# A macaron encoder layer on one core: the start of the program laid out anew, and a gate's result kept in the tile of its first product

## The chip, the cores and the metric

The kernel runs on one core of one Trainium2 chip. The metric is device microseconds of one execution, from the first to the last instruction plus what lies around them. The engines are named as the profile names them: PE is TensorE's matmul, PEld its weight load, DVE is VectorE, ACT is ScalarE, POOL is GpSimd and SP is SyncE. SP, ACT and POOL also issue the DMA transfers.

## What is computed

```python
def rmsnorm(x, g):
    y = x * lax.rsqrt(jnp.mean(x * x, axis=-1, keepdims=True) + NORM_EPS)
    return y * g

def swiglu(x, w_gate, w_up, w_down):
    return (jax.nn.silu(x @ w_gate) * (x @ w_up)) @ w_down

# one layer, x is 1024 tokens by 1024, float32
h = swiglu(rmsnorm(x, ffn1_pre_g), ffn1_w_gate, ffn1_w_up, ffn1_w_down)   # 2816 wide
x = x + 0.5 * rmsnorm(h, ffn1_post_g)
h = rmsnorm(x, mix_pre_g)
q, k, v = heads(h @ w_qkv)
o = concat(rmsnorm(neighbourhood_attention(...)), rmsnorm(dilated_attention(...)))
x = x + rmsnorm(o @ w_out, mix_post_g)
h = swiglu(rmsnorm(x, ffn2_pre_g), ffn2_w_gate, ffn2_w_up, ffn2_w_down)
x = x + 0.5 * rmsnorm(h, ffn2_post_g)
```

## The kernel before, in words

**Products.** Every float32 product is done as three fp32r products: each operand is split into a rounded part "hi" (a cast on ACT, L355 for weights, L171 for activations) and the rest "lo" (a subtraction on DVE, L356 and L172), and PE adds hi by hi, hi by lo and lo by hi (mm3, L262 to L264). On top of that the big products use a scheme with seven block products in the place of eight. The activations are cut into token halves and model halves (A11 and so on), and sums and differences of the blocks (S1 to S4 on the activations, T1 to T4 on the weights) are formed on DVE. A block product of one chunk is 12 matmuls: four slices of 128 by three products, 512 tokens wide.

**The first feed-forward net.** PairGemm walks over 22 pairs, each 128 columns of the gate matrix and 128 of the up matrix. The first `early` of them (9 in FFN1, 10 in FFN3, which is the second feed-forward net) have their two left products, A11 and A12, done ahead (`ahead`), while the second token half is still being normalised; the partial results go to DRAM through POOL's queue (s1d L428, sgd L543) and come back later. Then `run` takes one pair, b, per turn.

**A plain turn of `run`**, that is one with b at or over `early`, goes like this on PE, whose order is the written one: A11 of b (12 matmuls into bank a); then the last product of b-1, A22 (`last`, L518); then S2 of b, added into the same bank a, from which ACT must first have copied the A11 result (`keep`, L374, tile "s1" of pool sp); then A12 of b, whose result goes to `GatePairs.first`; then S1, S3 and S4. Pool sp has two buffers for the tag "s1". `first` (L533) takes a fresh tile "sg" from pool cp (tag "g1", three buffers, L549), adds A12 and s1 into it on DVE (L537) and applies SiLU on ACT (L539). `second` multiplies (L553) and writes the tile to DRAM (L560). `last` does the same for the other token half (SiLU L565, product L566) and, for odd b, forms four sums out of the tiles of b-1 and b (L574 to L577), of which L576 overwrites the sg tile of b-1 and L577 that of b; five POOL DMAs (L572, L579) then write the blocks to DRAM, in the order A22, S1, S3, S2, S4. S2 lies in the tile of b-1, S4 in that of b.

**Other traffic in a plain turn.** SP loads the weights of the pair after next (L349, L350) and a tile for sums of the down matrix (L318, L319); those sums are formed on DVE (L327 to L329) and written through POOL (L330), one step a turn in the turns 8 to 18.

**The start.** Token tiles 0 to 3 are loaded (L1374), the norm weights are spread to 128 partitions by a POOL DMA (L256), ACT squares and sums (L162), DVE forms the inverse root by three Newton steps from an integer guess (L137 to L148), scales whole tiles of 1024 (L211), PE transposes (L170), and the first product A11 is done for two pairs, in halves of 256 tokens. In this stretch PE, ACT and DVE go in the written order; afterwards only PE does, and a scheduler orders the others.

Of the kernel before, what the change touches and what calls it, by code (L numbers as in the profile page):

```python
# [10 lines left out]
F32 = mybir.dt.float32  # L11
F32R = mybir.dt.float32r
I32 = mybir.dt.int32
AF = mybir.ActivationFunctionType
# [5 lines left out]
P, T = 128, 512  # L20
# [73 lines left out]
class Weights:  # L94
# [64 lines left out]
def sumsq(c, x, ss, junk=None):  # L159
    if junk is None:  # L160
        junk = c.xp.tile([P, T], mybir.dt.bfloat16, tag="junk", name="junk", bufs=1)
    c.nc.scalar.activation(junk[:, :x.shape[-1]], x, AF.Square, accum_out=ss)  # L162
# [12 lines left out]
class Operand:  # L175
# [158 lines left out]
class PairGemm:  # L334
# [190 lines left out]
class GatePairs:  # L525
# [237 lines left out]
    return onehot, lncount, m.reshape(P, 384)  # L763


def build_bias(c, rel, t5, onehot, lncount):

    nc = c.nc
    stk = c.dr.tile([8, 8, 15, 24], F32, name="stk")
    tab = c.dr.tile([2, 8, T], F32, name="tab")  # L770
    t5t = c.bp.tile([32, 8], F32, tag="b0", name="t5t")
    nc.gpsimd.dma_start(t5t, t5.rearrange("h b -> b h"))
    for i in range(2):
        oh = c.bp.tile([P, T], F32, tag="oh", name="oh")
        cols = slice(511 * i, 511 * i + 511)
        nc.gpsimd.dma_start(oh[:32, :511], onehot[:, cols])
        lc = c.bp.tile([P, T], F32, tag="lc", name="lc")
        nc.gpsimd.dma_start(lc[:8, :511], lncount[:, cols].broadcast_to([8, 511]))
        ps = c.pst.tile([P, 4, P], F32, tag="tr", name="tabp").rearrange("p a b -> p (a b)")
        nc.tensor.matmul(ps[:8, :511], t5t, oh[:32, :511], start=True, stop=True)  # L780
        nc.vector.tensor_add(lc[:8, :511], ps[:8, :511], lc[:8, :511])
        nc.gpsimd.dma_start(tab[i, :, :511], lc[:8, :511])
        g = c.gab[i]
        dst = bass.AP(tensor=g.tensor, offset=g.offset, ap=[[P * 640, 8], [641, P], [1, 511]])
        nc.gpsimd.dma_start(dst, tab[i, :, :511].unsqueeze(1).broadcast_to([8, P, 511]))
    neg = c.bp.tile([P, T], F32, tag="oh", name="neg")
    nc.gpsimd.memset(neg[:, :384], NEG)
    nc.gpsimd.dma_start(c.nb.rearrange("h p r e -> p h (r e)"), neg[:, :384].unsqueeze(1).broadcast_to([P, 8, 384]))
    for cc in range(8):
        nc.gpsimd.dma_start(stk[cc], rel[:, :, 7 - cc:31 - cc])  # L790
    for r in range(16):
        r0 = min(max(r - 4, 0), 8)
        nc.gpsimd.dma_start(c.nb[:, r * 8:r * 8 + 8, r0:r0 + 8, :].rearrange("h c r e -> c h (r e)"),
                            stk[:, :, r0 - r + 7:r0 - r + 15, :].rearrange("c h r e -> c h (r e)"))
# [76 lines left out]
class Unit:  # L871
# [21 lines left out]
    def copy(self):  # L893
        c = self.c
        self.pt = c.ptp.tile([P, 4, P], F32, tag="pt", name="pt")
        (c.nc.vector.tensor_copy if self.count % 4 == 3 else c.nc.scalar.copy)(self.pt[:, :self.n], self.tps[:, :self.n])
# [232 lines left out]
class GroupNorm:  # L1129
# [48 lines left out]
def layer(tc, a, out):  # L1178
    nc = tc.nc
    c = Ctx(tc)  # L1180
    with ExitStack() as ctx:
# [184 lines left out]
        with ExitStack() as order:  # L1366
# [4 lines left out]
            def load(ts, queues):  # L1371
                for t, q in zip(ts, queues):
                    xs[t] = c.xp.tile([P, D], F32, tag="x", name="x", bufs=4)
                    q.dma_start(xs[t], x0[t])  # L1374
            xs = {}
            load((0, 1), (nc.sync, nc.scalar))
            op0 = Operand(c, load_gain(c, a["ffn1_pre_g"], "pre"), 0)

            def begin(pg):
                load((2, 3), (nc.scalar, nc.sync))  # L1380

                def drain():
                    while c.sums:
                        c.sums.popleft()()

                def norm(*ts):
                    op0.scale(*n[ts])
                    drain()
                def junk():
                    return c.xp.tile([P, D], F32, tag="s", name="junk", bufs=2)  # L1390
                n = {(0, 1): op0.squares([0, 1], [xs[0], xs[1]], junk())}
                norm(0, 1)
                pg.split_left(0)
                n[2, 3] = op0.squares([2, 3], [xs[2], xs[3]], junk())
                op0.one(0)
                op0.one(1)
                pg.split_left(1)
                acc, s1 = [pg.bank() for _ in range(2)], []
                for b in range(2):
                    pg.mm(acc[b], pg.w[b], 0, A11, cols=slice(0, 256))  # L1400
                op0.one(0)
                norm(2, 3)
                op0.one(2)
                op0.one(3)
                for b in range(2):
                    pg.mm(acc[b], pg.w[b], 0, A11, cols=slice(256, 512))
                    s1.append(pg.save(b, acc[b]))
                    if b:
                        op0.one(1)
                load((4, 5), (nc.gpsimd, nc.gpsimd))  # L1410
                op0.one(2)
                op0.one(3)
                order.close()
                order.enter_context(ordered())
                return s1
            F = lambda *ts: lambda: op0.norm(ts, [xs[t] for t in ts])
# [45 lines left out]
            vp.run(2, 3)  # L1462
            pg.fetch(0)
            pg.fetch(1)
            build_bias(c, a["na_rel_bias"], a["t5_rel_bias"], a["onehot"], a["lncount"])
            vp.run(4, 5)
            pg.begin()
            pg.begin_rest()
# [222 lines left out]
```

## Time and profile before

| | |
|---|---|
| median of 3 runs | 1920.19 us (1920.02 to 1921.11) |
| profiled execution | 1922.76 us, of which the span of instructions is 1921.0 us |
| granted TensorE clock, mean | 0.989 |
| PE busy | 1851.7 us, 96% |
| DVE / ACT / POOL busy | 1313.9 / 799.8 / 311.7 us |
| HBM read / written | 274.84 / 129.50 MB |

A row of a timeline gives start, duration, engine, line, operation, tile written and tiles read, shapes, and in brackets how long the engine sat idle before it and what ended that. A row of a stretch ("A:B") gives its length, then the busy time of PE, PEld, DVE, ACT and POOL with the number of instructions, the granted TensorE clock as a share, the busy share of the DMA engines and GB/s. A DMA row gives the tiles, the queue, the count, the size of one and the us from issue to landing.

### The profile page before, as it was taken

How to read it: one execution, taken by the hardware profiler on the slowest of the kernel's cores; microseconds unless marked ns; L12 is line 12 of the kernel's file. 1: busy time of each engine (PE TensorE's matmuls, PEld its weight loads, DVE VectorE, ACT ScalarE, POOL GpSimd, SP SyncE). 2: the span in 40 equal slices, each digit the busy share in tenths (PEclk: the TensorE clock that was granted, in tenths of full speed). 3: DMA queues.
4: the chain of work that ended last, by engine and by line, in shares of the span. 5: the costliest groups of instructions: out<-in, count | busy, mean ns of one | idle time of the engine just before them, and what ended most of it. 6: DMA issues, size and time to landing. Idle time of an engine off the chain costs nothing.

```text
span 1921.0 us, 25047 instructions
## 1 busy us (share of the span) xinstructions
PE 1851.7 (96%) x9044; PEld 1545.2 (80%) x9044; DVE 1313.9 (68%) x2205; ACT 799.8 (42%) x1287; POOL 311.7 (16%) x504
## 2 busy tenths in 40 slices
PE   5999999999999989999999999989999999999997
PEld 4788888888888867778799987777888888888886
DVE  5778777676565866548566775776788777654557
ACT  4522333334444545224477765453222333344332
POOL 2111111111000122342432310121111111110000
PEclk8999999999999999999999999999999999999999
DMA  6645465645986756866974642483456655476563
GB/s 237 223 159 188 170 222 216 222 167 197 327 273 200 273 193 205 292 198 197 313 265 142 212 159 88 155 301 136 159 192 241 215 195 210 159 275 212 198 229 133
DMA packets 162461, 400.96 MB, mean 209 GB/s; under 512 B 18001, under 2 KB 34561, under 8 KB 160289
## 3 DMA queue, kind: packets, MB, share of 16 engines
q1 hardware_dynamic: 112880, 224.62, 35.3%
q0 software_dynamic: 48592, 172.64, 24.8%
q10 hardware_dynamic: 864, 2.10, 0.3%
q8 instruction: 71, 1.16, 0.2%
q14 instruction: 54, 0.43, 0.1%
HBM read 274.84 MB, written 129.50 MB: 210 GB/s over the span
## 4 chain that ended last, share of the span: by engine, by line
PE 82%; DVE 6%; issue 5%; DMA 4%; ACT 2%; POOL 1%; SPq 0%; DVEq 0%; POOLq 0%; ACTq 0%
PE mmp L264 16%; PE mmp L262 16%; PE mmp L263 16%; PE accp L263 8%; PE accp L262 8%; PE accp L264 8%; PE po L992 3%; PE ptp L891 2%; PE sp L980 2%; PE trp L170 1%; PE po L1113 1%; DMA wraw<-in_wqk_dram 1%; PE sp L1100 1%; DMA x<-x 1%; DMA wraw<-in_wu_dram 1%
## 5 line engine op out<-in xcount | busy, mean ns | idle before, releaser
L262 PE MATMUL mmp<-x,whi 128*128 128x512 f32 (+1 forms) x1464 | 579.8, 396 | 7.6 <-ACT whi L355 3.6
L264 PE MATMUL mmp<-x,wlo 128*128 128x512 f32 (+1 forms) x1464 | 575.5, 393 | 1.0 <-DVE wlo L356 1.0
L263 PE MATMUL mmp<-x,whi 128*128 128x512 f32 (+1 forms) x1464 | 574.8, 393 | 0.5 <-DVE x L172 0.2
L262 PEld LDWEIGHTS mmp<-x,whi 128*128 128x128 f32 x1464 | 278.2, 190 | 67.0 <-ACT whi L355 4.2
L264 PEld LDWEIGHTS mmp<-x,wlo 128*128 128x128 f32 x1464 | 277.9, 190 | 62.3 <-DVE wlo L356 1.9
L263 PEld LDWEIGHTS mmp<-x,whi 128*128 128x128 f32 x1464 | 278.4, 190 | 59.9 <-DVE x L172 1.4
L613 DVE TENSOR_TENSOR pw<-praw,pw 128x1024 fp32r<-128x1024 f32 (+1 forms) x182 | 199.2, 1138 | 122.4 <-ACT pw L612 122.1
L612 ACT CAST pw<-praw 128x1024 fp32r<-128x1024 f32 (+1 forms) x182 | 169.2, 983 | 208.6 <-PE accp L264 168.0
L355 ACT CAST whi<-wraw 128x1024 fp32r<-128x1024 f32 x129 | 135.2, 1050 | 251.6 <-PE mmp L263 213.0
L262 PE MATMUL accp<-pw 128*128 128x512 f32 x600 | 234.4, 391 | 0.0
L264 PE MATMUL accp<-pw 128*128 128x512 f32 x600 | 233.5, 389 | 0.0
L263 PE MATMUL accp<-pw 128*128 128x512 f32 x600 | 233.4, 389 | 0.0
L356 DVE TENSOR_TENSOR wlo<-wraw,whi 128x1024 fp32r<-128x1024 f32 x129 | 157.6, 1225 | 23.6 <-ACT whi L355 23.5
L264 PEld LDWEIGHTS accp<-pw 128*128 128x128 f32 x600 | 112.6, 188 | 23.7
L262 PEld LDWEIGHTS accp<-pw 128*128 128x128 f32 x600 | 112.7, 188 | 23.5 <-issue 0.4
L263 PEld LDWEIGHTS accp<-pw 128*128 128x128 f32 x600 | 112.7, 188 | 23.0
L560 POOL DMA_DIRECT2D g<-sg x44 | 23.9, 542 | 475.2 <-DVE sg L553 304.0
L518 DVE TENSOR_TENSOR c<-mmp,u 128x512 f32<-128x512 f32 x52 | 36.0, 691 | 83.9 <-PE mmp L264 82.8
L374 ACT COPY s<-mmp 128x512 f32<-128x512 f32 x52 | 30.5, 587 | 147.3 <-PE mmp L264 145.7
L355 ACT CAST whi<-traw 128x512 fp32r<-128x512 f32 x52 | 32.3, 621 | 118.2 <-DVE traw L444 59.2
L172 DVE TENSOR_TENSOR x<-trp,x 128x512 fp32r<-128x512 f32 x84 | 57.2, 687 | 34.7 <-ACT x L171 34.7
L443 DVE TENSOR_TENSOR wraw<-wraw 128x1024 f32<-128x1024 f32 x52 | 63.6, 1224 | 24.2 <-DMA wraw<-in_wqk_dram 11.9
(230 smaller groups left out, 2699.8 us busy)
## 6 DMA issues: line engine op xcount, KB each, us to landing
praw<-g SPq DMA_DIRECT2D x70, 512.0 KB
wraw<-in_wg_dram SPq DMA_DIRECT2D x44, 512.0 KB
wraw<-in_wu_dram SPq DMA_DIRECT2D x44, 512.0 KB
tr<-in_wd_dram SPq DMA_DIRECT2D x44, 512.0 KB
g<-sg POOLq DMA_DIRECT2D x88, 256.0 KB, 4.1
ts<-tr POOLq DMA_DIRECT2D x22, 1024.0 KB, 4.7
praw<-ts SPq DMA_DIRECT2D x88, 256.0 KB
praw<-in_wd_dram SPq DMA_DIRECT2D x66, 256.0 KB
```

What stands on the lines that cost most here:

```text
L172: nc.vector.tensor_sub(lo, ps, hi.bitcast(F32))
L262: nc.tensor.matmul(out, ahi, bhi, start=start, stop=False, skip_group_check=go_on)
L263: nc.tensor.matmul(out, ahi, blo, start=False, stop=False, skip_group_check=go_on)
L264: nc.tensor.matmul(out, alo, bhi, start=False, stop=stop, skip_group_check=go_on)
L355: nc.scalar.copy(hi, raw)
L356: nc.vector.tensor_sub(lo, raw, hi.bitcast(F32))
L443: nc.vector.tensor_sub(r[:, 0:2], r[:, 1:3], r[:, 0:2])
L612: nc.scalar.copy(w[side][:, 0, :m], raw[:, :m])
L613: nc.vector.tensor_sub(w[side][:, 1, :m], raw[:, :m], w[side][:, 0, :m].bitcast(F32))
L891: c.nc.tensor.transpose(self.tps[:, j, :], self.probs[:, j * P:(j + 1) * P], c.ident)
L980: nc.tensor.matmul(out, lhs, keys[i], start=i == 0, stop=i == 1)
L992: nc.tensor.matmul(po[0][:, un * 2 + j], u.pt[:, 2 * j + t, :], rhs, start=t == 0, stop=t == 1)
```

## The change

Three things are altered.

1. The start is written out anew (`begin`). The norm weights come as one row of 4 KB and PE spreads them over the partitions by a product with a row of ones (L1402); one of the first two tiles is squared and summed on DVE instead of ACT (L1409); the inverse root is ACT's square root, DVE's reciprocal and one Newton step (L1419 to L1424); tiles are scaled by halves of 512; weights of three pairs instead of two come by halves on SP's queue; three pairs instead of two have their A11 product done here; and the order of PE, ACT and DVE is written down. Token tiles 4 and 5 now come on SP's queue, the copies of xn to DRAM are issued at the end, and the loads of the neighbourhood bias (stk) move from build_bias to turn 1.
2. FFN1 does 10 pairs ahead instead of 9, and the steps of the second token half move one turn later with it.
3. `GatePairs.first` uses the tile s1, where it is given one, as the result tile: `sg = s1 or ...`. It is given one for the pairs begun in the start and in every plain turn of FFN1 and FFN3.

```diff
@@ PairGemm.ahead
             if b + 1 not in self.w:
-                self.split_left(b + 1)
+                if b + 1 == len(begun):
+                    c.behind(lambda: self.split_left(b + 1), DVE, ACT)
+                else:
+                    self.split_left(b + 1)
@@ GatePairs.first
     def first(self, b, ps, keep, s1=None):
         c, nc = self.c, self.c.nc
-        sg = c.sp.tile([P, T], F32, tag="s1", name="sg") if keep else self.tile()
+        sg = s1 or (c.sp.tile([P, T], F32, tag="s1", name="sg") if keep else self.tile())
         if s1 is not None:
             nc.vector.tensor_add(sg, ps, s1)
@@ build_bias
-    stk = c.dr.tile([8, 8, 15, 24], F32, name="stk")
+    stk = c.rel
-    for cc in range(8):
-        nc.gpsimd.dma_start(stk[cc], rel[:, :, 7 - cc:31 - cc])
@@ ffn
-                pg.start()
@@ layer, the start
-            load((0, 1), (nc.sync, nc.scalar))
-            op0 = Operand(c, load_gain(c, a["ffn1_pre_g"], "pre"), 0)
+            op0 = Operand(c, None, 0)
             def begin(pg):
...
+                nc.sync.dma_start(row[:1, :D], a["ffn1_pre_g"])
+                load((0, 1), (nc.sync, nc.scalar))
+                fetch(0, 0)
                 load((2, 3), (nc.scalar, nc.sync))
+                for b, i in ((1, 0), (2, 0), (0, 1), (1, 1), (2, 1)):
+                    fetch(b, i)
+                nc.vector.memset(row[:1, D:], 1.0)
+                nc.vector.memset(eps, EPS)
+                nc.scalar.activation(ss[:, 2:3], eps[:, 0:1], AF.Sqrt)
+                for g, copy in enumerate((nc.scalar.copy, nc.vector.tensor_copy)):
+                    ps, sl = pg.bank(), slice(g * T, g * T + T)
+                    nc.tensor.matmul(ps, row[:1, D:], row[:1, sl], start=True, stop=True)
+                    copy(op0.gain[:, sl], ps)
...
+                def square_here(t):
+                    nc.vector.tensor_tensor_reduce(out=xn[t], in0=xs[t], in1=xs[t], scale=1.0, scalar=0.0,
+                                                   op0=ALU.mult, op1=ALU.add, accum_out=ss[:, t:t + 1])
+                def root(t):
+                    x = ss[:, t:t + 2]
...
+                    nc.scalar.activation(q, x, AF.Sqrt, bias=eps[:, 0:1], scale=1.0 / D)
+                    nc.vector.tensor_scalar(h, x, -0.5 / D, -0.5 * EPS, op0=ALU.mult, op1=ALU.add)
+                    nc.vector.reciprocal(y, q)
+                    nc.vector.tensor_mul(e, y, h)
+                    nc.vector.tensor_mul(e, e, y)
+                    nc.vector.scalar_tensor_tensor(y, e, 1.5, y, op0=ALU.add, op1=ALU.mult)
...
+                square(0)
+                square_here(1)
+                root(0)
+                whigh(0, 0)
+                scale(0, 0)
+                scale(1, 0)
+                turn(0, 0)
+                turn(1, 0)
...
+                products(2, (2,), every)
+                low(3, 1)
+                wlow(0, 1)
+                s1.append(pg.save(2, acc[2]))
+                for b in (1, 2):
+                    whigh(b, 1)
+                    wlow(b, 1)
+                save(0, 1, 2, 3)
+                pg.fetch_left(3)
+                pg.fetch_left(4)
...
-            op, fin, hs, prep = ffn(1, op0, prep, gate_pairs(1, op0, a["wg1"], a["wu1"], 9), get1,
-                                    {0: [F(4, 5), L(6, 7)], 2: [U(4)], 3: [F(6, 7), U(5)], 5: [U(6)], 6: [U(7)]},
+            op, fin, hs, prep = ffn(1, op0, prep, gate_pairs(1, op0, a["wg1"], a["wu1"], 10), get1,
+                                    {0: [lambda: c.behind(F(4, 5), ACT), L(6, 7)], 1: [rel], 3: [U(4)], 4: [F(6, 7), U(5)], 6: [U(6)], 7: [U(7)]},
```

How the order moves. On ACT, from turn 11's copy of v to turn 12's, before: s_2308 is the copy of A11 of b = 12, c_2322 the SiLU in `last` of b = 11, u_2355 the copy after S2. "waits" names what an instruction waits for; the DMASW entries are transfers that POOL issued.

```order
L374 COPY v<-mmp 128x512 [waits PE_49]
L355 CAST whi<-traw 128x512 [waits DVE_49,Activation_49]
L355 CAST whi<-wraw 128x1024 [waits DMAHW6_49,PE_49,Activation_49]
L374 COPY s_2308<-mmp 128x512 [waits PE_49]
L355 CAST whi<-wraw 128x1024 [waits DVE_49,PE_49,Activation_49]
L565 ACTIVATE c_2322<-c_2322 128x512 [waits DVE_49]
L374 COPY u_2355<-mmp 128x512 [waits PE_49]
```

The same stretch now, in which s_2340 is the copy of A11 of b = 12 and c_2354 the SiLU in `last` of b = 11:

```order
L374 COPY v<-mmp 128x512 [waits PE_49]
L355 CAST whi<-traw 128x512 [waits DVE_49,Activation_49]
L355 CAST whi<-wraw 128x1024 [waits DMAHW5_49,PE_49,Activation_49]
L355 CAST whi<-wraw 128x1024 [waits DVE_49,PE_49,Activation_49]
L568 ACTIVATE c_2354<-c_2354 128x512 [waits DVE_49]
L374 COPY s_2340<-mmp 128x512 [waits DMASW2_49,DVE_49]
L374 COPY u_2387<-mmp 128x512 [waits PE_49]
```

The copy has moved behind the SiLU of the pair before, and it waits for a DVE instruction and for a POOL transfer. The copies of b = 14, 16, 18 and 20 in FFN1, and of b = 12 to 20 by twos in FFN3, stand the same way; those of odd b stand where they stood.

On POOL, the writes that end the pair of b = 10 and 11, and the first ones after them, before (sg is the tile from pool cp):

```order
L572 DMA g_6_169<-c_2267 128x512 [waits DMASW0_49,DVE_49]
L579 DMA g_2_165<-s_2334 128x512 [waits DMASW1_49,DVE_49]
L579 DMA g_5_168<-c_2133 128x512 [waits DMASW2_49,DVE_49]
L579 DMA g_1_164<-sg 128x512 [waits DMASW3_49,DVE_49]
L579 DMA g_3_166<-sg 128x512 [waits DMASW4_49,DVE_49]
```

and now, where s_2064 and s_2207 are the A11 copies of b = 10 and 11:

```order
L575 DMA g_6_163<-c_2299 128x512 [waits DMASW7_49,DVE_49]
L582 DMA g_2_159<-s_2366 128x512 [waits DMASW0_49,DVE_49]
L582 DMA g_5_162<-c_2166 128x512 [waits DMASW1_49,DVE_49]
L582 DMA g_1_158<-s_2064 128x512 [waits DMASW2_49,DVE_49]
L582 DMA g_3_160<-s_2207 128x512 [waits DMASW3_49,DVE_49]
```

The writes stand in the same order; the fourth and fifth now read the tiles of tag "s1". A POOL transfer takes the numbered slot whose last use it waits for, so DMASW2, for which s_2340 waits, is the write of s_2064.

More of the change, by code (lines that the diff above doesn't have):

```diff
@@ L1375, in layer @@
             xs = {}
-            load((0, 1), (nc.sync, nc.scalar))
-            op0 = Operand(c, load_gain(c, a["ffn1_pre_g"], "pre"), 0)
+            op0 = Operand(c, None, 0)
             def begin(pg):
-                load((2, 3), (nc.scalar, nc.sync))
[L1382 to L1412, printed above, removed]
@@ new lines, in begin, with fetch @@
+                row, eps, ss = c.xp.tile([P, D + P], F32, tag="s", name="row", bufs=2), *[
+                    c.small.tile([P, 4], F32, tag=t, name=t) for t in ("eps", "ss")]
+                raw, xn, got, acc, s1 = [None] * 3, [None] * 4, {}, [], []
+                def fetch(b, i):
+                    if raw[b] is None:
+                        where = dict(tag="x1", bufs=c.deep) if b == 2 else dict(tag="g")
+                        raw[b] = (c.xp if b == 2 else c.wg).tile([P, 2, T], F32, name="graw", **where)
+                        pg.w[b] = [c.wr.tile([P, 2, T], F32R, tag="g" + p, name="w" + p) for p in ("hi", "lo")]
+                    nc.sync.dma_start(raw[b][:, i], pg.srcs[b][0][:, i * T:(i + 1) * T])
@@ new lines, in begin @@
+                nc.sync.dma_start(row[:1, :D], a["ffn1_pre_g"])
+                load((0, 1), (nc.sync, nc.scalar))
+                fetch(0, 0)
+                load((2, 3), (nc.scalar, nc.sync))
+                for b, i in ((1, 0), (2, 0), (0, 1), (1, 1), (2, 1)):
[3 more added lines that the diff above has]
+                nc.scalar.activation(ss[:, 2:3], eps[:, 0:1], AF.Sqrt)
+                op0.gain = c.xp.tile([P, D], F32, tag="pre", name="gain", bufs=1)
@@ new lines, in place @@
+                def place(t):
+                    where = dict(tag="x1", bufs=c.deep) if t == 3 else dict(tag="xn", bufs=c.xn)
+                    xn[t] = c.xp.tile([P, D], F32, name="xn", **where)
+                def root(t):
+                    x = ss[:, t:t + 2]
+                    q, h, y, e = [c.small.tile([P, 4], F32, tag=n, name=n)[:, :2] for n in ("q0", "v", "y", "e")]
+                    nc.scalar.activation(q, x, AF.Sqrt, bias=eps[:, 0:1], scale=1.0 / D)
[4 more added lines that the diff above has]
+                    nc.vector.scalar_tensor_tensor(y, e, 1.5, y, op0=ALU.add, op1=ALU.mult)
+                    r.update({t + i: y[:, i:i + 1] for i in range(2)})
@@ new lines, in begin, with scale, save, turn @@
+                r = {}
+                def scale(t, g):
+                    sl = slice(g * T, g * T + T)
+                    nc.vector.scalar_tensor_tensor(xn[t][:, sl], xs[t][:, sl], r[t], op0.gain[:, sl],
+                                                   op0=ALU.mult, op1=ALU.mult)
+                def save(*ts):
+                    for t in ts:
+                        nc.gpsimd.dma_start(op0.saved[t], xn[t])
+                def turn(t, g):
+                    got[t, g] = ps = c.pst.tile([P, 4, P], F32, tag="tr", name="trp")
+                    for j in range(4):
+                        nc.tensor.transpose(ps[:, j, :], xn[t][:, g * T + j * P:g * T + j * P + P], c.ident)
@@ new lines, in operand, with high, low, whigh @@
+                def operand(t, g):
+                    return [h[:, :, t * P:t * P + P] for h in op0.x[A12 if g else A11]]
+                def high(t, g):
+                    nc.scalar.copy(operand(t, g)[0], got[t, g])
+                def low(t, g):
+                    hi, lo = operand(t, g)
+                    nc.vector.tensor_sub(lo, got[t, g], hi.bitcast(F32))
+                def whigh(b, i):
+                    nc.scalar.copy(pg.w[b][0][:, i], raw[b][:, i])
+                def wlow(b, i):
+                    hi, lo = [h[:, i] for h in pg.w[b]]
+                    nc.vector.tensor_sub(lo, raw[b][:, i], hi.bitcast(F32))
@@ new lines, in products @@
+                def products(b, kinds, cols):
+                    if b == len(acc):
+                        acc.append(pg.bank())
+                    for kind in kinds:
+                        w, x = pg.w[b][kind == 2], op0.x[A11][kind == 1]
+                        for k in range(4):
+                            nc.tensor.matmul(acc[b][:, cols], w[:, 0, k * P:k * P + P], x[:, k, cols],
+                                             start=kind == 0 and k == 0, stop=kind == 2 and k == 3)
+                first, second, every = slice(0, 256), slice(256, 512), slice(0, 512)
@@ new lines, in begin @@
+                place(0)
+                place(1)
+                square(0)
[6 more added lines that the diff above has]
+                turn(1, 0)
+                square(2)
+                high(0, 0)
+                wlow(0, 0)
+                high(1, 0)
+                low(0, 0)
+                square(3)
+                low(1, 0)
+                root(2)
+                whigh(1, 0)
@@ new lines, in begin @@
+                place(2)
+                place(3)
+                products(0, (0, 1, 2), first)
+                scale(2, 0)
+                scale(3, 0)
+                products(1, (0,), first)
+                turn(2, 0)
+                wlow(1, 0)
+                products(1, (1,), first)
+                turn(3, 0)
+                products(1, (2,), first)
+                for t in (2, 3):
+                    high(t, 0)
+                    low(t, 0)
+                products(0, (0, 1, 2), second)
@@ new lines, in begin @@
+                whigh(2, 0)
+                scale(0, 1)
+                load((4,), (nc.sync,))
+                scale(1, 1)
+                load((5,), (nc.sync,))
+                turn(0, 1)
+                s1.append(pg.save(0, acc[0]))
+                high(0, 1)
+                scale(2, 1)
+                low(0, 1)
+                products(1, (0, 1, 2), second)
+                turn(1, 1)
+                high(1, 1)
+                scale(3, 1)
+                s1.append(pg.save(1, acc[1]))
@@ new lines, in begin @@
+                low(1, 1)
+                wlow(2, 0)
+                products(2, (0,), every)
+                turn(2, 1)
+                high(2, 1)
+                low(2, 1)
+                products(2, (1,), every)
+                turn(3, 1)
+                whigh(0, 1)
+                high(3, 1)
+                products(2, (2,), every)
[5 more added lines that the diff above has]
+                    wlow(b, 1)
@@ L1464, in layer @@
             pg.fetch(1)
[L1465 removed]
+            build_bias(c, a["t5_rel_bias"], a["onehot"], a["lncount"])
             vp.run(4, 5)
```

8 lines of the change are left out of this document (7 added, 1 removed).

## Prediction

> **What bounds the kernel now.** First the page: PE is busy in nearly all of the span. Then the stretches of 50 us, to see where it is not.
>
> ```profile
> span 1921.0 us, 25047 instructions
> PE 1851.7 (96%) x9044; PEld 1545.2 (80%) x9044; DVE 1313.9 (68%) x2205; ACT 799.8 (42%) x1287; POOL 311.7 (16%) x504
> 0.00:50.00 50.00, 28.30 (x127) 23.31 (x128) 25.65 (x58) 21.95 (x33) 13.30 (x29) 0.90 0.69 243
> 300.00:350.00 50.00, 50.00 (x220) 40.97 (x219) 36.34 (x44) 17.95 (x25) 5.33 (x9) 1.00 0.60 213
> 1600.00:1650.00 50.00, 50.00 (x219) 40.92 (x218) 34.91 (x42) 15.95 (x22) 6.62 (x11) 1.00 0.57 202
> ```
>
> In the first 50 us PE stands idle for 50 - 28.30 = 21.7 us; in the feed-forward nets it is full, and whatever makes it wait there lengthens the span by as much. The timeline of PE says where the 21.7 us lie.
>
> ```profile
> 11.96 2.22 PE L170 MATMUL trp<-ident,xn 128*128 128x128 f32 x8 [11.96 <-DVE xn L211]
> 14.85 0.58 PE L262 MATMUL mmp<-x,whi 128*128 128x256 f32 x1 [0.68 <-ACT x L171]
> 16.17 0.41 PE L262 MATMUL mmp<-x,whi 128*128 128x256 f32 x1
> 16.38 0.41 PE L263 MATMUL mmp<-x,whi 128*128 128x256 f32 x1
> 20.65 0.90 PE L170 MATMUL trp<-ident,xn 128*128 128x128 f32 x4
> 27.61 2.28 PE L170 MATMUL trp<-ident,xn 128*128 128x128 f32 x8 [6.06 <-DVE xn L211]
> 30.57 0.58 PE L262 MATMUL mmp<-x,whi 128*128 128x256 f32 x1 [0.68 <-ACT x L171]
> 35.26 0.28 PE L264 MATMUL mmp<-x,wlo 128*128 128x256 f32 x1
> 35.38 0.27 PE L262 MATMUL mmp<-x,whi 128*128 128x256 f32 x1
> 35.73 1.03 PE L170 MATMUL trp<-ident,xn 128*128 128x128 f32 x8
> 34.80:35.00 0.20, 0.20 (x3) 0.20 (x2) 0.00 (x0) 0.00 (x0) 0.07 (x1) 0.74 0.00 0
> ```
>
> 18 of them are the two waits for scaled tiles; the rest are waits under 1.1 us. PE is also slow there: matmuls of 256 tokens follow each other by 0.21 us, and by 0.12 from 34.9 on, where the last row shows the granted clock leave 0.50. Eight transposes took 2.2 us against 1.03. With 20 transposes and some 42 matmuls at the slow pace that is 3.0 + 3.9 = 7 us. So the start loses 21.7 + 7 = 28.7 us of PE.
>
> **The start, part by part.** DVE's first scaling and the gain's landing, with the prices for what is new:
>
> ```profile
> 10.53 2.48 DVE L211 SCALAR_TENSOR_TENSOR xn<-x,y,gain 128x1024 f32<-128x1024 f32 x2 [0.44 <-DMA gain<-in_ffn_pre_g_dram]
> 5.38 1.06 ACT L162 ACTIVATE junk<-x 128x1024 f32<-128x1024 f32 x1 [2.43 <-DMA x<-in_x_dram]
> 9.92 0.16 DVE L148 SCALAR_TENSOR_TENSOR y<-e,y 128x2 f32<-128x2 f32 x1
> L780 PE MATMUL tabp<-oh,t5t 32*8 32x511 f32 x4 | 1.9, 588 | 0.0
> L896 DVE COPY pt<-ptp 128x512 f32<-128x512 f32 x16 | 11.0, 690 | 1.1
> L1158 DVE SCALAR_TENSOR_TENSOR og<-og,y,gd 128x512 f32<-128x512 f32 x16 | 11.8, 746 | 0.0
> 20.99 1.04 ACT L355 CAST whi<-graw 128x1024 fp32r<-128x1024 f32 x1 [5.25 <-DMA graw<-in_wg_dram]
> ```
>
> - Spread gain: the POOL DMA of 512 KB goes. The row of 4 KB should land by about 2.8 us (estimate: half of the 5.38 at which the first 512 KB tile is there). Full float32 matmuls as at L780 come as two instructions each, four in 1.9 us; at half clock two gain products take some 3.5 us, to 6.3, and DVE's copy 0.69, to 7.0.
> - Sum of squares on DVE: no row shows it; a pass over 1024 costs 2.48 / 2 = 1.24 us, twice that if it took two passes. I take 1.24: 8.3.
> - Root: twelve small DVE steps of 0.2 us are replaced by a square root on ACT and five steps, 1.0 us: 9.3. Scaling a half costs 0.75: the first transpose at 10.2 instead of 11.96.
> - With the written order, root, scaling and transposes of tiles 2 and 3 run under the first products, so the 6.06 us go; the clock has to rise once, not twice.
> - What is late next: weights of pair 3. Their load waits, by the order in `begin`, for the buffer of pair 0, whose second half is split at about 28.4 us. Landed, cast (1.04) and subtracted behind twelve root steps and a scaling on DVE, they hold PE for about 2.3 us near 34. Short waits at hand-overs between PE, ACT and DVE add 1.8 (five of 0.2 to 0.7, like the 0.68 above).
>
> PE idle then comes to 10.2 + 2.3 + 1.8 = 14.3 us, and the slow pace to 3.8 (12 transposes and about 22 matmuls, 1.8 + 2.0): 18.1 lost instead of 28.7. **The start gains 10.6 us**, with 7 to 13 for the unknown sum of squares, the landing of pair 3 and where the clock rises. The tenth pair ahead moves 24 matmuls, adds three DVE additions and two reloads; PE at 50.00 of 50 covers them, 2 us uncovered. The bias loads of 11 KB move from idle POOL time to idle POOL time: nothing.
>
> **The plain turns.** `sg = s1` is not only for the start. In every plain turn the tile of "s1", of which there are two, now lives on as the gate's result until the pair's last sums are written to DRAM. For even b the next copy into that buffer must wait for the write of S2 of the pair before, and S2's products on PE, added into the bank that is being copied, stand behind it. One such place today (ACT, DVE, POOL, then the landing of that write):
>
> ```profile
> 315.47 0.59 ACT L374 COPY s<-mmp 128x512 f32<-128x512 f32 x1 [4.64 <-PE mmp L264]
> 318.21 0.69 DVE L518 TENSOR_TENSOR c<-mmp,u 128x512 f32<-128x512 f32 x1 [2.26 <-PE mmp L264]
> 318.98 0.63 ACT L565 ACTIVATE c<-c 128x512 f32<-128x512 f32 x1
> 320.25 0.69 DVE L566 TENSOR_TENSOR c<-c,c 128x512 f32<-128x512 f32 x1
> 322.42 0.69 DVE L576 TENSOR_TENSOR sg<-s,sg 128x512 f32<-128x512 f32 x1
> 323.41 0.54 POOL L579 DMA_DIRECT2D g<-sg  x1 [0.18 <-issue]
> g<-sg POOLq DMA_DIRECT2D x1, 256.0 KB, 9.4
> ```
>
> Today the copy starts at 315.47, long done when A22 of the pair before ends at 318.2 and PE goes on. In the changed program that same A22 first has to pass through subtraction, SiLU, product and the sums on DVE until 323.1, and S2 is issued at 323.41 and lands 9.4 us later, at 332.8. Then the copy, 0.59, and hand-overs of 0.08: PE goes on at 333.5 and not at 318.2, a stall of 15.3 us. Nothing covers it: PE's order is written, with no other product before S2, and behind the copy on ACT stand only steps that need S2. From issue to the end of A22 it is 323.41 - 318.2 = 5.2, so each stall is 5.2 + 0.67 + landing = 5.9 + landing.
>
> There are five such turns in each net (b = 12, 14, 16, 18, 20). Landings of that write today, in those ten turns in order of time:
>
> ```profile
> g<-sg POOLq DMA_DIRECT2D x1, 256.0 KB, 8.5
> ...
> g<-sg POOLq DMA_DIRECT2D x1, 256.0 KB, 8.2
> g<-sg POOLq DMA_DIRECT2D x1, 256.0 KB, 2.9
> g<-sg POOLq DMA_DIRECT2D x1, 256.0 KB, 8.6
> ...
> g<-sg POOLq DMA_DIRECT2D x1, 256.0 KB, 9.6
> g<-sg POOLq DMA_DIRECT2D x1, 256.0 KB, 2.6
> 320.36 0.55 SPq L349 DMA_DIRECT2D wraw<-in_wg_dram  x1
> 322.26 0.45 SPq L350 DMA_DIRECT2D wraw<-in_wu_dram  x1
> ```
>
> In full 8.5, 9.4, 8.2, 8.2, 2.9 and 8.6, 8.3, 8.4, 9.6, 2.6. The eight long ones share the DMA engines with loads of weights that SP issues at 320.36 to 322.26 in the same turn, before the write. These loads hang on DVE's work after A22 and not on S2, so they will be there in the stall as well: I keep today's landings. Eight stalls of 5.9 + 8.65 = 14.5 and two of 5.9 + 2.75 = 8.6 make **133 us**.
>
> After each stall the clock has to rise again: the start shows it lowered after a wait of 6.06 us, and 4.3 us of matmuls (30.57 to 34.9) at 0.21 for 0.12, 44% lost; the unbroken slow row before that lasted 6.7 us (14.85 to 21.55). That is 1.9 to 2.9 us, 2.4 in the middle: **24 us** for ten, with 0 and 30 as ends. On this the Trainium skill, "TensorE: Matmul & The Clock Gate" (Part 1: The HAM clock gate), says that an idle window of about 3.4 us halves the clock and about 3.4 us of sustained work restores it, in a free-running window. Reckoned by its 3.4 us the ten cost 15 us, an estimate; the trace's 4.3 and 6.7 us decide.
>
> **The sum.** 1921.0 - 10.6 + 133 + 24 = 2067.4 us of span. The profiled execution has 1.76 us around its span (1922.76), and the median of the three runs is 1920.19; from the median the sum gives 1920.2 + 146.4 = **2067 us**.
>
> **The rivals.**
>
> - *Fast landings.* While PE waits no other work of the turn starts, so the write might land as in the two quiet turns, in 2.6 to 2.9 us. Then each stall is 8.6 us: 1920.2 - 10.6 + 86 + 24 = 2020. Against it: the competing loads are issued before the write. The Trainium skill, "DMA: Bandwidth & Descriptors" (Anatomy of one DMA), gives about 2.0 us plus bytes at 436 GB/s, 2.6 us for 256 KB, an estimate; the two quiet turns agree (2.9, 2.6), the eight loaded ones do not (8.2 to 9.6). Chance 7%.
> - *The other side: the copy finds its buffer free.* If the wait in the order is met before A22 of b-1 ends, at 318.2 in the example, PE never sees it and only the start counts: 1920.2 - 10.6 = 1910, faster. For that S2's write would have to land 14.6 us sooner than today, or the tile be taken from another buffer. For it: the copy's wait lists names and no times. Against it: the sums that overwrite the tile need A22 themselves. It decides at a landing before the end of A22. Chance 6%.
> - *The start gains nothing*, since the loads of pair 3 come late as they did before (20.99, after 5.25 us of ACT's wait): the stalls stay, 1920.2 + 157 = 2077. It lies within the range.
>
> **How the numbers follow.** Forecast with the stalls at today's landings: 86%, and alone 2045 to 2085 (landings a microsecond either way are 10 us, the clock 0 to 30, the start 3). Fast landings 7%, no stall 6%, the rest 1%. The range reaches down to the fast landings, 2015 to 2085, and leaves out the case of no stall and some of the forecast's own tails. A measurement of this kernel can tell about 0.2%, 4 us: faster 0.06, same 0.01, slower 0.93.
>
> **What would show it.** Right: in the plain turns the copy into "s1" of every second turn waits for a POOL write, 14 us of PE idle with ACT named behind it, ten times, and the granted clock dips after each; PE idle in the first 50 us near 14 us; first transposes at about 10 us. Wrong: PE at 50.00 of 50 between 250 and 450 us, or waits of 8 us in turns with loads, or a first transpose after 12 us.

## The result, and the profile after

The changed kernel takes 2063.0 us (median of 4 runs, 2059.4 to 2066.8) where the kernel before took 1920.1 in the same session: a ratio of 1.0751, interval 1.0731 to 1.0770. It is slower by 143 us, and the forecast was 2067.

The page of the changed kernel answers the first rows of before. The profiled execution took 2059.4 us.

```profile
span 2057.6 us, 25076 instructions
PE 1871.4 (91%) x9048; PEld 1556.9 (76%) x9048; DVE 1316.1 (64%) x2206; ACT 799.2 (39%) x1290; POOL 310.4 (15%) x503
```

Two things stand in the PE row. Its share fell from 96 to 91%: PE is idle for 186 us where it was idle for 69. And its busy time rose by 20 us with four instructions more, so some matmuls ran slower. The stretches of 50 us say where; the columns are as before.

```profile
0.00:50.00 50.00, 38.41 (x171) 29.68 (x172) 33.36 (x69) 27.47 (x46) 13.69 (x30) 0.97 0.72 262
300.00:350.00 50.00, 35.83 (x150) 28.87 (x149) 24.45 (x30) 11.53 (x16) 5.30 (x9) 0.86 0.44 163
1600.00:1650.00 50.00, 35.87 (x147) 28.91 (x147) 24.23 (x30) 11.53 (x16) 5.30 (x9) 0.86 0.44 163
```

PE is busy ten microseconds longer in the first 50 us (38.41 for 28.30), of which 3.75 are the new products that spread the norm weights. The plain turns of both feed-forward nets, where PE was at 50.00 of 50, lose 14 us in each 50, at a granted clock of 0.86. The chain of one such loss, from the timelines of ACT, POOL and PE, with the landing of the write:

```profile
303.09 0.59 ACT L374 COPY s<-mmp 128x512 f32<-128x512 f32 x1 [4.64 <-PE mmp L264]
330.29 0.54 POOL L582 DMA_DIRECT2D g<-s  x1 [0.18 <-issue]
g<-s POOLq DMA_DIRECT2D x1, 256.0 KB, 8.2
338.59 0.58 ACT L374 COPY s<-mmp 128x512 f32<-128x512 f32 x1 [12.10 <-DMA g<-s]
339.23 0.80 PE L262 MATMUL mmp<-x,whi 128*128 128x512 f32 x1 [14.17 <-ACT s L374]
339.83 0.63 PE L263 MATMUL mmp<-x,whi 128*128 128x512 f32 x1
...
342.39 0.41 PE L263 MATMUL mmp<-x,whi 128*128 128x512 f32 x1
342.64 0.39 PE L264 MATMUL mmp<-x,wlo 128*128 128x512 f32 x1
```

The copy at 303.09 belongs to an odd b: it waits for its own product only. The copy at 338.59 belongs to an even b, and its row names a transfer of a tile g, the write of S2. That was issued at 330.29 and landed 8.2 us later, at 338.5; the copy starts at once, and PE goes on at 339.23 after 14.17 us. Behind that the matmuls follow each other by 0.43 us and not 0.23 until 342.4. The waits of PE say how often, as sum, times and longest:

```profile
PE mmp L262 <- ACT s L374: 131.8, 10, 14.2
PE trp L170 <- DVE x L172: 12.9, 9, 3.4
PE mmp L262 <- ACT whi L355: 6.2, 3, 2.6
```

### The profile page after: what moved, and what is told of

Its sections match the earlier page's. It is cut to its first block, busy times and chain, and to the rows that moved or that the text cites. A ratio compares the mean times of both kernels' runs of the same rounds, so it can differ in the third digit from the quotient of the medians.

```text
span 2057.6 us, 25076 instructions
## 1 busy us (share of the span) xinstructions
PE 1871.4 (91%) x9048; PEld 1556.9 (76%) x9048; DVE 1316.1 (64%) x2206; ACT 799.2 (39%) x1290; POOL 310.4 (15%) x503
## 4 chain that ended last, share of the span: by engine, by line
PE 45%; issue 36%; DMA 7%; DVE 5%; POOL 4%; ACT 2%; SPq 0%; POOLq 0%; DVEq 0%; ACTq 0%
PE accp L263 7%; PE accp L264 7%; PE accp L262 7%; PE mmp L264 5%; PE mmp L262 5%; PE mmp L263 5%; PE po L993 3%; PE ptp L892 2%; POOL g L582 2%; DMA tr<-in_wd_dram 2%; PE sp L981 1%; PE po L1114 1%; PE trp L170 1%; DMA ts<-tr 1%; DVE pw L616 1%
## 5 line engine op out<-in xcount | busy, mean ns | idle before, releaser
L262 PE MATMUL mmp<-x,whi 128*128 128x512 f32 x1444 | 581.5, 403 | 140.0 <-ACT s L374 131.8
L264 PE MATMUL mmp<-x,wlo 128*128 128x512 f32 x1444 | 574.9, 398 | 1.7 <-DVE wlo L356 1.6
L263 PE MATMUL mmp<-x,whi 128*128 128x512 f32 x1444 | 574.3, 398 | 0.2 <-DVE x L1450 0.2
L540 DVE TENSOR_TENSOR s<-mmp,s 128x512 f32<-128x512 f32 x27 | 18.7, 691 | 186.9 <-PE mmp L264 186.9
L563 POOL DMA_DIRECT2D g<-s x24 | 13.0, 541 | 438.8 <-DVE s L556 420.7
L446 DVE TENSOR_TENSOR wraw<-wraw 128x1024 f32<-128x1024 f32 x52 | 63.6, 1223 | 20.4 <-DMA wraw<-in_wqk_dram 9.9
```

The lines of the kernel that those rows point to most:

```text
L262: nc.tensor.matmul(out, ahi, bhi, start=start, stop=False, skip_group_check=go_on)
L263: nc.tensor.matmul(out, ahi, blo, start=False, stop=False, skip_group_check=go_on)
L264: nc.tensor.matmul(out, alo, bhi, start=False, stop=stop, skip_group_check=go_on)
L446: nc.vector.tensor_sub(r[:, 0:2], r[:, 1:3], r[:, 0:2])
```

## The experiments

The theory was that the reuse of s1 in the plain turns is the whole loss, by ten waits for the landing of a write and a clock that falls after each, and that the new start gains about 10 us. The rivals were that the start, the tenth pair or an order changed behind them loses the time; that the reuse costs by something else than its buffer; and, on the sizes, that PE's extra busy time is not the clock and that the landing is long for another reason than SP's loads.

**Own tile.** The plain turns get a fresh tile again, the pairs done ahead keep the reuse:

```diff
-        sg = s1 or (c.sp.tile(...) if keep else self.tile())
+        sg = (s1 if keep else None) or (c.sp.tile(...) if keep else self.tile())
```

> The changed program, but a plain turn takes a fresh tile for the gate's result again; only the pairs done ahead keep s1 as the result tile. Theory (the reuse in the plain turns is the whole loss, and the new start gains): the 131.8 us of PE waiting for ACT's copy L374 go, with the some 20 us of PE time lost to the lowered clock; 1920 less the start's gain of 10.6 gives about 1909, between 1907 and 1913. Rival (the new start, the tenth pair or a changed order after it loses the time): about 2060 still.

Measured: 1908.3 us (1906.8 to 1910.8), 0.9937 of before (0.9924 to 0.9950). The theory's value. Its page and one plain stretch:

```profile
span 1906.5 us, 25082 instructions
PE 1851.1 (97%) x9048; PEld 1544.6 (81%) x9048; DVE 1315.6 (69%) x2206; ACT 799.4 (42%) x1290; POOL 310.4 (16%) x503
300.00:350.00 50.00, 50.00 (x219) 40.96 (x218) 36.35 (x45) 17.03 (x23) 6.62 (x11) 1.00 0.51 188
```

PE has the same 9048 instructions as in the changed kernel and is busy 20.3 us less. The two profiled spans differ by 151.1, and the waits behind the copy (131.8) and this busy time (20.3) make 152.1: nothing else of size is left. This version beats both kernels.

**The line alone.** The kernel before with only the changed line of `first`.

> The program before with one line of the change, the result of the gate kept in the tile s1 where there is one. Theory: ten stalls as in the changed program, 133 us of waiting and 20 to 24 of clock, with the old start: 2063 + 10.6, about 2073. Rival (the reuse only hurts together with the new start and ten pairs ahead): about 1920.

Measured: 2073.1 us, 1.0794 of before (1.0772 to 1.0815), the value that was expected, which was the changed kernel's time and the 10.6 us of the start. The line needs neither the new start nor the tenth pair to do its harm; its waits of PE begin

```profile
PE mmp L262 <- ACT s L374: 133.4, 10, 14.6
PE trp L170 <- DVE xn L211: 18.3, 2, 11.9
```

with the ten stalls of the changed kernel and the two long waits of the old start.

**Three buffers.** The reuse stays, and the copy finds a third buffer:

```diff
-        s = self.c.sp.tile([P, T], F32, tag=tag, name=tag)
+        s = self.c.sp.tile([P, T], F32, tag=tag, name=tag, bufs={"s1": self.c.n1, "v": self.c.nv}.get(tag))
...
+            c.n1, c.nv = 3, 1
```

> The changed program with the reuse kept, but three buffers for the tag s1 in the turns instead of two (and one for v, to make room). Theory (the copy waits for a buffer, and nothing else is wrong with the reuse): the copy into s1 meets a buffer that was free a turn ago, no stall, about 1909. Rival (what costs is that the addition is done in place, or where the result lies): about 2060 still.

Measured: 1908.7 us, 0.9938 (0.9924 to 0.9952), with one buffer for v in the place of two. The addition in place and the place of the result cost nothing; what was missing is one buffer of 256 KB. In its waits of PE the copy doesn't occur.

**Stalls filled with work.** PE repeats the twelve matmuls of A12 during the stall, into the bank that A12 overwrites afterwards.

```diff
+                pb = self.bank()
+                if b % 2 == 0 and b >= self.early + 2:
+                    ...
+                    for k in range(16 if b < self.n - 2 else 8):
+                        mm3(c, pb, hi[:, 1, sl], ...)
                 self.mm(a, w[T2], 0, S2, True)
                 u2 = self.keep(a, "u2")
-                pb = self.bank()
```

> The changed program, but in the ten stalled turns PE repeats the twelve matmuls of A12 ahead of S2, four times (twice in the last), into a bank that A12 itself overwrites later: 10.9 us of extra work in a stall of some 13. Theory (the some 20 us by which PE's busy time grew are matmuls at the lowered clock after each stall): the clock stays up, the stalls end when they did, and 108 more us of PE work make the program faster, about 2063 - 20 = 2043. Rival (the extra PE time has another cause): 2060 or more. Rival (the stall is not a wait but work that PE is short of): about 2063 + 100.

Measured: 2063.2 us, no gain, where 2043 was expected; by the time alone the rival (another cause) fits as well. The filling did not prolong the program, so PE was in fact waiting and not short of work; but the clock fell all the same. The waits and the timeline of PE, at the stall that was shown above:

```profile
PE mmp L262 <- ACT s L374: 32.5, 10, 4.8
339.88 0.50 PE L262 MATMUL mmp<-x,whi 128*128 128x512 f32 x1 [3.07 <-ACT s L374]
340.22 0.39 PE L263 MATMUL mmp<-x,whi 128*128 128x512 f32 x1
...
341.14 0.42 PE L264 MATMUL mmp<-x,wlo 128*128 128x512 f32 x1
341.38 0.61 PE L262 MATMUL mmp<-x,whi 128*128 128x512 f32 x1
...
344.78 0.41 PE L264 MATMUL mmp<-x,wlo 128*128 128x512 f32 x1
```

3.07 us of idleness were left. The first matmuls behind it still run at full pace, and then, from 341.38 to 344.78, at half. By the spacing of matmuls (what is over the usual 0.2335 us from one to the next, in the 16 us after a stall) the ten stalls lose 18.0 us here and 19.3 in the changed kernel. The test had left too much idle time to tell the cause of the extra busy time, so it was made again with more filling:

```diff
-                    for k in range(16 if b < self.n - 2 else 8):
+                    for k in range(19 if b < self.n - 2 else 11):
```

> The changed program with the stalls filled up further than before: 57 repeated matmuls in each (33 in the last of a net) instead of 48 (24), so that PE stands idle for about 1 us where 3.1 us were left. With 48 the clock still fell after each stall, by 18 us of PE time in all against 19.3 without any. Theory (an idle stretch of 3 us is already long enough to lower the clock, one of 1 us is not): the clock stays up and the time falls by 16 to 18 us, about 2046, though PE works 130 us more. Rival (the clock falls for another reason, such as the start of a new bank or a load on the chip): 2063.

Measured: 2047.3 us, 1.0666 of before (1.0635 to 1.0697), 16 us faster than the changed kernel with 522 matmuls more. The waits, and the stretch of FFN1's plain turns:

```profile
PE mmp L262 <- ACT s L374: 12.3, 10, 2.7
250.00:500.00 250.00, 244.72 (x1057) 197.89 (x1056) 133.16 (x160) 63.28 (x86) 25.23 (x43) 1.00 0.40 146
```

The granted clock of 250 to 500 us is 1.00, where it was 0.88 in the changed kernel (a share over all the time, that of the stalls too: from 331 to 339 us, in the stall shown, it is 0.50), and the ten stalls lose 2.6 us to slow matmuls and not 19.3. The extra busy time is the clock.

**What makes the landing long.** Three runs. First the order of the writes, so that S2 goes first:

```diff
-        for k, v in ((S1, s1), (S3, a21), (S2, a11), (S4, a12)):
+        for k, v in ((S2, a11), (S4, a12), (S1, s1), (S3, a21)):
```

> The changed program with the four sums of a pair written in the order S2, S4, S1, S3 instead of S1, S3, S2, S4, so that 512 KB less of POOL's own writes stand before the one that PE waits for. Theory (the landing is set by the loads of weights that SP has issued before it): S2 is still formed third, so its issue moves by 0.2 us only and its landing little: 0.2 to 1 us for each of ten stalls, 2050 to 2061. Rival (the landing is set by POOL's own writes ahead of it): it falls from 8.5 to about 5 us, ten times 3.5, about 2028.

Measured: 2065.7 us, the ten waits 132.6. This run tells nothing: POOL's order isn't the written one, and the scheduler put S1 and S3, whose sums are ready sooner, ahead again in all stalled turns.

Then fewer loads in those turns:

```diff
-            one_a_turn(sums, NF, NF - 3 - len(sums))
+            one_a_turn(sums, NF, 0)
```

> The changed program with the sums of the down matrix done in turns 0 to 11 and not 8 to 18, so that 1 MB of the 2 MB that SP loads in a stalled turn are gone from there. Theory (SP's loads set the landing of S2): halfway from 8.65 to the 2.75 us of the turns without loads, 2.9 us for each of eight stalls, about 2040. Rival (POOL's own writes set it): 2060.

Measured: 2114.4 us, 1.1016 (1.0982 to 1.1050), 51 us slower than the changed kernel. The forecast of the total (2040) failed, the part that was meant to be tested came out: its waits of PE, then one of the waits of DVE that the second one hangs on.

```profile
PE mmp L262 <- ACT s L374: 115.3, 10, 12.7
PE mmp L262 <- DVE v L492: 31.9, 8, 6.0
PE mmp L262 <- ACT whi L355: 17.4, 5, 5.7
DVE tr L327 <- DMA tr<-in_wd_dram: 46.9, 12, 6.2
```

The stalls fell from 14.1 to 12.0 us, three quarters of what was expected, and S2 landed in 6.8 us in the first and in 5.9 to 6.1 us in the seven others. But the sums now stand in the turns of the pairs done ahead, whose own tiles are read back as well; DVE stands at L327 until the load of the down matrix lands (and 37.7 us in all at L446, for loads of weights), and u2 and v (L484, L492), for which PE waits, are queued behind it.

Last, the weights of the pair after next wait for S2 itself:

```diff
+                if b >= 11 and b % 2:
+                    self.fetch(b + 3, self.sink.g[S2][b // 2])
...
+            if behind is not None:
+                nc.sync.dma_start(r[:, 0:2, :1], behind[:, :2].unsqueeze(2))
```

> As the run with fewer loads, and the remaining loads of weights of those turns wait, by a copy of some bytes of S2 into their tile, until S2 has landed; nothing else competes with the write then. Theory (SP's loads set the landing): it falls to about 2.7 us as in the turns without loads, 5.9 us less for each of eight stalls, about 2015, the case of fast landings in the prediction. Rival (POOL's own writes set it): no faster than the run with fewer loads, about 2060.

Measured: 2089.5 us, 1.0884 (1.0848 to 1.0919), 25 us faster than the run that it builds on. It is still far from the 2015 expected, since what that run had lost in the earlier turns stays: PE waits for v for 31.5 us here as well. The waits, the landing of S2 and one stall:

```profile
PE mmp L262 <- ACT s L376: 88.8, 10, 10.3
g<-s POOLq DMA_DIRECT2D x1, 256.0 KB, 2.7
358.78 0.80 PE L262 MATMUL mmp<-x,whi 128*128 128x512 f32 x1 [8.67 <-ACT s L376]
```

With POOL's own three writes still ahead of it, S2 lands in 2.7 us and the stall is 8.67. So it is SP's loads that make the landing long, not POOL's writes. (The step before this one took also a POOL write of 1 MB, the sums of the down matrix, out of these turns; in the changed kernel that write was issued at 323.14 and landed in 4.6 us, before S2 was issued at 330.29.) The Trainium skill, "DMA: Bandwidth & Descriptors" (Queues, rings and completion order), says that each DMA engine goes round the queues it has work for, a packet at a time; 8.2 us beside 2 MB of SP's loads, 6.0 beside 1 MB and 2.7 without any agree with that.

**The start.** Four variants of the version with its own tile (1908.3), to see which part of the start gains. Nine pairs ahead instead of ten:

```diff
-gate_pairs(1, op0, a["wg1"], a["wu1"], 10)
+gate_pairs(1, op0, a["wg1"], a["wu1"], 9)
```

> The version that takes its own tile in the plain turns (1908.3), with nine pairs ahead in the first net instead of ten. Theory (the tenth pair costs and brings nothing, as the prediction had it): 1908, within 3. Rival (a part of the 12 us gained comes from the tenth pair): 1911 to 1920.

The norm weights by POOL's DMA again, in the place of the row and the two products:

```diff
-                    nc.tensor.matmul(ps, row[:1, D:], row[:1, sl], start=True, stop=True)
-                    copy(op0.gain[:, sl], ps)
+                gain = load_gain(c, a["ffn1_pre_g"], "pre")
```

> The version that takes its own tile (1908.3), with the norm weights spread by a POOL DMA of 512 KB as before, in the place of the row and the two products. Theory (the gain's landing is on the path of the start: before it landed at 10.5 and the first scaling began then, in the changed program at 8.9 or so): the first transposes come 1 to 2 us later, about 1910. Rival (the landing is hidden behind the squares and the root): 1908 or, with the 3.75 us of gain products gone from PE, no less.

The second half of pair 0 split sooner, so that pair 3's weights are fetched 11 us sooner:

```diff
                 whigh(1, 0)
+                whigh(0, 1)
...
                 wlow(1, 0)
+                wlow(0, 1)
+                pg.fetch_left(3)
```

> The version that takes its own tile (1908.3), with the second half of pair 0's weights split right after the root of tiles 2 and 3, where ACT and DVE stand idle, so that pair 3's load is issued at about 18.5 us instead of 29.3. Theory (the load sets PE's wait of 2.85 + 0.52 us near 37 us and the lowered clock after it): the cast then stands behind the squares of tiles 4 and 5 and a SiLU, done at about 35.5 instead of 37.4: 2 us less, 1906; with the clock staying up another 1.6 less. Rival (the load is not what is last): 1908.

And the same with tiles 4 and 5 normalised behind pair 3's weights:

```diff
-{0: [lambda: c.behind(F(4, 5), ACT), L(6, 7)], 1: [rel], 3:
+{0: [L(6, 7)], 1: [rel], 2: [lambda: c.behind(F(4, 5), ACT)], 3:
```

> As the run with pair 3's load earlier, and the squares and the scaling of tiles 4 and 5 begin two turns later, behind the split of pair 3's weights. Theory: the cast is done by 34.5, the wait of 3.4 us and the lowered clock after it (1.6 us) are gone: 1903 to 1904. Rival (tiles 4 and 5 are now late and hold PE at their transposes): 1906 to 1912.

Measured in this order: 1910.7 (0.9962 of before, 0.9947 to 0.9978), 1910.3 (0.9956, 0.9939 to 0.9974), 1909.1 (0.9957, 0.9941 to 0.9973) and 1908.0 (0.9953, 0.9938 to 0.9967). The intervals overlap, with each other and with the version's own: the times don't tell the four apart. The 1908.3 is from another session, whose kernel before took 1920.7 against 1918.5 here, so the times themselves can't be set against it either; the 1906 and the 1903 to 1904 that were expected of the last two were not reached. Where the trace tells them apart, it does so at the start. First PE's wait for pair 3's weights in the version with its own tile, with the ten microseconds behind it:

```profile
37.48 0.50 PE L262 MATMUL mmp<-x,whi 128*128 128x512 f32 x1 [2.85 <-ACT whi L355]
38.74 0.50 PE L264 MATMUL mmp<-x,wlo 128*128 128x512 f32 x1 [0.52 <-DVE wlo L356]
40.00:50.00 10.00, 10.00 (x43) 8.12 (x42) 8.00 (x14) 7.03 (x11) 4.29 (x8) 0.86 0.86 277
```

The same with pair 3's load earlier:

```profile
34.15 0.50 PE L262 MATMUL mmp<-x,whi 128*128 128x512 f32 x1 [0.98 <-ACT whi L355]
36.10 0.50 PE L264 MATMUL mmp<-x,wlo 128*128 128x512 f32 x1 [1.22 <-DVE wlo L356]
40.00:50.00 10.00, 10.00 (x53) 8.08 (x51) 8.93 (x22) 7.18 (x12) 3.79 (x7) 1.00 0.85 300
```

The wait of 2.85 became one of 0.98 and the clock stays up, 53 matmuls in the ten microseconds and not 43. That the shorter wait is the reason is likely and not shown: in the run with nine pairs the clock stayed up behind a wait of 2.50 at the same place. With tiles 4 and 5 later the first of the waits is gone altogether, but their transposes wait, as the rival had it:

```profile
35.62 0.50 PE L264 MATMUL mmp<-x,wlo 128*128 128x512 f32 x1 [1.45 <-DVE wlo L356]
43.54 0.63 PE L170 MATMUL trp<-ident,xn 128*128 128x128 f32 x4 [1.12 <-DVE xn L211]
49.38 1.04 PE L170 MATMUL trp<-ident,s 128*128 128x128 f32 x4 [2.00 <-DVE x L172]
```

With the gain by DMA the first transposes come at 11.20, against 9.97 to 11.09 in the other three variants and the version itself: 0.1 to 1.2 us, less than the 1 to 2 expected.

## Why the prediction was right, point by point

**The start (forecast: 10.6, between 7 and 13).** The version with its own tile is 1908.3 against 1920.7, 12 us (0.50 to 0.76% by the interval, 9.6 to 14.6). Step by step, from the timelines of PE, DVE and ACT of the changed kernel:

```profile
3.28 3.75 PE L1402 MATMUL mmp<-row 1*128 1x512 f32 x4 [3.28 <-DMA row<-in_ffn_pre_g_dram]
7.67 1.22 DVE L1409 CUSTOM_DVE_ANT_0 xn<-x 128x1024 f32<-128x1024 f32 x1
11.01 1.94 PE L1440 MATMUL trp<-ident,xn 128*128 128x128 f32 x8 [3.98 <-DVE xn L1430]
36.82 0.50 PE L262 MATMUL mmp<-x,whi 128*128 128x512 f32 x1 [2.60 <-ACT whi L355]
38.08 0.50 PE L264 MATMUL mmp<-x,wlo 128*128 128x512 f32 x1 [0.53 <-DVE wlo L356]
```

The row landed at 3.28 (forecast 2.8; 2.2 to 3.4 in the other runs), the gain products took 3.75 (3.5), the sum of squares 1.22, one pass (1.24), the first transposes came at 11.01 (10.2), and pair 3's weights held PE for 3.1 us (2.3). What was late next was named rightly; that this wait would lower the clock once more was not foreseen; the row of 40 to 50 us of the version with its own tile, above, shows it. Added up as in the prediction, PE lost 11.6 us idle and 3.75 in the gain products (14.3 forecast for both), about 3 at the slow pace (3.8) and 1.5 at the second lowering (nothing): 20 instead of 18.1, so a gain of about 9 us by 50 us, an estimate, and not 10.6. The slow pace has to be read from the spacing of the matmuls: the granted clock reads 1.00 from 15 to 20 us before, although the matmuls of 256 tokens follow each other by 0.21 there.

Not all of the 12 us was seen to arise in the start. The first product of the down matrix of FFN1 begins at 469.4 us before, at 461.2 and 459.0 in the runs with their own tile and with three buffers: 8.2 and 10.4 us of gain by then. The two programs are alike in the start, and their 2.2 us stand already at the wait for pair 3's weights, 37.48 against 35.32, of which 1.1 came with the landing of the row (3.36 and 2.27). The rest of the 12 lies behind, where the runs differ among themselves (last section). So the start gained 8 to 10 us, within the range that was given; that 12 came out on the other side of 10.6 says little.

**The tenth pair (forecast: 0).** Nine pairs took 0.9962 of before and ten 0.9937, in different sessions and with intervals that just overlap: 4.8 us between them. The other three variants of the session with nine pairs have ten and stand at 0.9953 to 0.9957, so most of this lies between the sessions. Not refuted, and not settled to better than some 5 us.

**The bias loads (forecast: 0).** The stage that they left, from the bias table to the first scores, lasted 152.3 us before, 146.6 with the line alone, where they have not moved, and 146.0 in the changed kernel. No effect can be seen, in a stage that varies by 6 us.

**The stalls (forecast: ten, 133 us).** Ten, 131.8 us, in the turns that were named. The form 5.9 + landing fits: 5.97 + 8.2 = 14.17 in the turn shown, 5.97 + 2.7 = 8.67 where the loads were held back. It fails in one turn, the last stalled one of FFN3: the stall was 10.34 and the landing 2.7, since POOL waited 2.09 us for DVE in the middle of its writes and S2 went out 1.7 us later. The same 2.09 stand in that turn before the change; the prediction reckoned its 5.2 us from another turn. That the loads would still be there in the stall was a choice of the prediction and turned out right; the rival of fast landings had its price right (8.6 a stall) and its condition wrong.

**The clock (forecast: 24, between 0 and 30).** 19.3 us by the spacing of matmuls, 20.3 by PE's busy time, 16 by the run that keeps the clock up. The mechanism is shown, the size was a fifth too high: a stall cost 1.4 to 2.7 us, 1.9 in the mean, and not 2.4. The slow matmuls behind the stall that is shown lasted 3.2 us (339.23 to 342.4), where the prediction took 4.3 and 6.7 from the start.

**The sum.** -12 + 131.8 + 20.3 = +140, measured +143. The waits and PE's busy time were read in the profiled execution, which at 2059.4 was the fastest of the four and 139 above before; the 3 us up to the median lie within the intervals. The forecast's +146.4 had the stalls 1 us too high, the clock 4 too high and the gain outside the stalls 1 or 2 too low. The rival in which the start gains nothing (2077) is out by the version with its own tile. The rival in which the copy finds its buffer free gives the time of the version with its own tile (1910 forecast, 1908.3 measured); it needed the tile from another buffer, and it did not happen by itself.

## What to carry to other kernels

A tile that is used in place lives until the last reader of its new content, and if that is a transfer to DRAM, the next user of its buffer waits for the landing: before saving a tile, ask who takes the buffer next and what stands behind that instruction on its engine. One buffer more, or the old tile, and a loss of 150 us is a gain of 12. And where PE has to wait for about 2 us or more, reckon with the clock: behind a wait of over 3.5 us it was always lowered here (the first 15 us apart), behind one of 1.8 to 3.5 us often and not always, and the price of a stall, 1.4 to 2.9 us, hardly depended on how long it was.

## What the runs showed of the hardware that was not expected

**The clock falls after short waits too.** Ten stalls of 8.7 to 14.2 us lost 19.3 us to slow matmuls; ten of 2.8 to 4.8 us lost 18.0. In the run with more filling nine stalls of 0.45 to 2.16 us lost 0.1 us each, and the one of 2.66 us lost 1.6. But the length alone doesn't decide. One wait of 1.82 us for a weight cast, behind the attention, stands in all fourteen profiled runs; in seven of them, the changed kernel among them, matmuls behind it ran at half pace, in the other seven at full. First the changed kernel, then the version with its own tile, each with the 4.5 us that begin 1.5 us after the wait, and at last a wait of 3.44 in the changed kernel that cost nothing:

```profile
1312.87 0.50 PE L262 MATMUL mmp<-x,whi 128*128 128x512 f32 x1 [1.82 <-ACT whi L355]
1314.37:1318.87 4.50, 4.50 (x14) 3.54 (x14) 4.08 (x15) 0.97 (x2) 0.09 (x1) 0.62 0.72 226
1241.46 0.50 PE L262 MATMUL mmp<-x,whi 128*128 128x512 f32 x1 [1.82 <-ACT whi L355]
1242.96:1247.46 4.50, 4.50 (x20) 3.63 (x20) 4.09 (x15) 1.68 (x3) 0.55 (x1) 1.00 0.70 238
1354.45 0.66 PE L170 MATMUL trp<-ident,s 128*128 128x128 f32 x4 [3.44 <-DVE x L172]
1354.45:1360.45 6.00, 6.00 (x30) 4.90 (x31) 5.76 (x15) 2.53 (x4) 0.54 (x1) 1.00 0.39 133
```

Behind the first 15 us every wait of over 3.5 us was followed by a lowered clock, in all runs. What decides between 1.8 and 3.5 us stays open. The slow stretch can begin late, 1.5 us after PE has gone on (339.88 to 341.38 above), and lasted 3.4 us there. The Trainium skill, "TensorE: Matmul & The Clock Gate" (HAM oscillation — how this bites in real kernels), warns of idle gaps over about 3.4 us; here 1.82 was enough in seven runs and too little in seven, and the runs decide.

**A landing depends on who loads beside it.** The same write of 256 KB took 8.2 us beside 2 MB of SP's loads, 6.0 beside half of them (one of eight: 6.8) and 2.7 beside none.

**One stage varies by itself.** From the bias table to the first scores the profiled runs took 145.9 to 152.3 us, without relation to the edits: 147.2 and 150.8 for the versions with their own tile and with three buffers, which differ in nothing there. With pair 3's load earlier, FFN1's down product began at 457.4 us, 1.6 to 3.8 sooner than without, and nothing of it was left at the end. Gains of 1 to 3 us in the start can be seen in the trace of the start and not in the time of this program; what makes the stage vary stays open.
